# A decoder layer on one core: output projection among the last attention head, cached keys from a later block on

## The chip, the core and the metric

The kernel runs on one core of one Trainium2 chip. The metric is the device time of one execution, in microseconds (us); lower is better. The engines are called PE (TensorE, matmuls), DVE (VectorE), ACT (ScalarE), POOL (GpSimd) and SP (SyncE, which here issues DMAs). Each runs its own instructions in order.

## The reference, cut

One layer of a hybrid decoder, all in float32. For 1,024 prompt tokens (with 16 learned tokens ahead of them), and for 8 decode tokens that each read 4,096 cached keys and values through a page table:

```python
proj = rms_norm(x, ln_mix_pre) @ w_in              # 1024 -> 2560 columns: q, k, v, a, g
u = a * sigmoid(g)
p = softmax(q @ k.T / 8 - slope * distance)        # causal, 4 heads, two maps each
o = (p[map 0] - lam * p[map 1]) @ v                # decode rows: k, v from cache_k, cache_v
conv = silu(layer_norm(causal_depthwise(u, 31)))
mix = concat(rms_norm(o), conv) @ w_out            # the output projection
x = x + rms_norm(mix)
f = (silu(h @ w_gate) * (h @ w_up)) @ w_down       # h = rms_norm(x), FFN width 2816
y = x + rms_norm(f)
```

## The kernel before, in words

Every float32 matmul of the prompt is made of three: operands are split into a rounded high part H and a rest L (`load_split`: a cast on ACT, a subtraction on POOL or DVE), and `mm3` (L148) issues H·H, H·L and L·H, lines 149 to 151.

The program is written as one stream, with the decode tokens' work strewn into the prompt's. Stages in order:

- Input projection (`stripe_ag`, `stripe_q`, `stripe_k`, `stripe_v`), by columns, with the convolution beside it on DVE, ACT and POOL.
- Attention, 32 blocks: `n = 0..31` is head `h = n // 8` and block `i = n % 8` of 128 queries. `attn` makes scores (tile `S`, L507 and L508), takes row minima on DVE (L509, into `nm`), exponentials on ACT (L515), joins the two maps on DVE (L526), transposes on PE (`AT`, L534), copies on ACT (`ats`, `metaT`, L538) and sums over values on PE (`o`, L548). After four blocks the group is normalized (`oh`, L557 to L566; `or` on POOL, L564), and `heads_out` transposes it (`oT`, L571) into `mo`, some blocks later, where `i % 4 == cfg["od"]`.
- Output projection, 8 blocks of 128 tokens. `w_out_load` splits the eight pieces of w_out (`wo0` to `wo7`; ACT cast L138, POOL subtraction L140), two per attention block from block `wo0` on. `c_load` loads a block's inputs (`mx`, `xr`), `c_block` splits them (`mH`, `mL`), runs 48 matmuls into the tiles `mo`, and normalizes. A block calls for `last_head`, the group of head 3 that holds its tokens. From attention block 24 + `c0` on, one output block follows each attention block.
- The FFN: 66 pieces of weights (`w_raw` loads, `w_split` splits: `wr`, `wH`, `wL`), gate, up and down matmuls (`pg`, `pu`, `dn`), the down sums gathered on DVE (L998).

The decode tokens' cached pages come in steps. A step is one pair of pages, 512 KB: a key step (`dec_scores`) loads it, multiplies by the query on POOL (L679) and, later, sums on DVE (L689, `head_sums`); a value step (`dec_values`) loads it for PE (`pv`, L731). There are 128 of each; the first 23 steps are keys, then both alternate. `head_sums` is placed behind a later product: `rlag` says how many products wait. After the 16 key steps of a decode row `dec_max` (DVE L697, L704, POOL L706) and, once `elag` more products are out, `dec_exp` (DVE L711) follow. The steps are dealt out by rates: `rate_b[h]` per attention block from block `db` on, `rate_c` per output block, `rate_d` per slot of the FFN (133 slots, `fill`). When they are through, the decode tokens' own projections (`sample_units`, 81 steps) take `rate_s` per slot.

Page pairs lie in two kinds of buffers. Before the FFN's part begins (`kv_n[1]` false) there are `kv` of them; then `kv` takes turns with the `p` buffers of attention:

```python
        if kv_n[1] and kv_n[0] % 7 < cfg["p"]:
            return slp.tile([P, NKEY], F32, tag="p", name=name, bufs=cfg["p"])
        return slp.tile([P, 1024], F32, tag="kv", name=name, bufs=cfg["kv"])
```

So six of seven go to the six `p` buffers, and each of these comes up again after seven calls.

The order of each engine is fixed when the program is built: a scheduler takes the written stream, its priorities (decode steps may go ahead by `behind`) and data dependences, and puts the instructions of each engine in one row. SP issues nearly all loads, in its own row.

## Time and profile before

| | |
|---|---|
| median of 3 runs | 1452.58 us (1447.33 to 1453.26) |
| the profiled execution, its own time | 1442.33 us |
| its span, first to last instruction | 1440.6 us |
| PE busy | 1353.5 us (94%) |
| DVE, POOL, ACT busy | 876.8, 560.5, 552.2 us |
| mean granted PE clock | 0.976 of full speed |
| DMA moved | 264.35 MB, 183 GB/s over the span |

All durations below come from the profiled execution, which is 10 us under the median of the runs. A matmul's busy time overlaps the next one's, so PE's time is read from where it is idle, and from the granted clock, 1 being the upper of two levels and a mean below 1 a mixture of both. Idle time of another engine matters only where PE waits for it. Names such as `k` or `wH` are the program's tiles; "<-" stands before what they are made from.

### The profile page before, as it was taken

What the parts mean: (1) busy time and instruction counts of PE and PEld (TensorE: products, weight loads), DVE (VectorE), ACT (ScalarE), POOL (GpSimd) and SP (SyncE); (2) the same over time, 40 slices, a digit from 0 to 9 for tenths busy, and PEclk for the clock granted to TensorE, in tenths of its full rate; (3) what the DMA queues carried; (4) which work ended last, traced back from release to release, by engine and by line L of the source; (5) the groups of instructions that cost most, each with busy time, mean ns of one, the idle gap of its engine ahead of it and who ended that gap; (6) DMA issues with size and microseconds to landing.
All of it is one profiled execution on the core that took longest, in us unless ns stands there. A gap on an engine that the chain in (4) does not pass through costs nothing.

```text
span 1440.6 us, 21580 instructions
## 1 busy us (share of the span) xinstructions
PE 1353.5 (94%) x6960; PEld 1054.5 (73%) x6960; DVE 876.8 (61%) x1403; ACT 552.2 (38%) x1112; POOL 560.5 (39%) x351
## 2 busy tenths in 40 slices
PE   5999899979858999999999989999999999999997
PEld 5999799978746787777777667677676765666666
DVE  5689996945765467465748366565754265462158
ACT  7566978697855345212222121222122112211122
POOL 4598866444444123545445455454530000000023
PEclk9999999999979999999999999999999999999999
DMA  8221024226515538678777868687687656664454
GB/s 253 78 59 39 28 64 145 81 88 199 160 61 183 176 125 283 221 241 278 260 244 235 260 202 262 229 273 248 206 267 231 224 159 217 220 202 125 146 190 176
DMA packets 199678, 264.35 MB, mean 183 GB/s; under 512 B 16423, under 2 KB 99816, under 8 KB 199557
## 3 DMA queue, kind: packets, MB, share of 16 engines
q1 hardware_dynamic: 188912, 254.40, 54.1%
q10 hardware_dynamic: 10653, 8.57, 1.9%
q8 instruction: 55, 0.90, 0.3%
q14 instruction: 58, 0.48, 0.1%
HBM read 245.92 MB, written 17.48 MB: 183 GB/s over the span
## 4 chain that ended last, share of the span: by engine, by line
PE 61%; DMA 2%; issue 2%; DVE 2%; SPq 2%; POOL 1%; ACT 0%; POOLq 0%; DVEq 0%; ACTq 0%
PE pg L149 5%; PE pu L149 5%; PE pg L150 5%; PE pu L150 5%; PE pu L151 5%; PE pg L151 5%; PE dn L149 5%; PE dn L150 5%; PE dn L151 5%; PE pv L731 4%; PE mo L151 2%; PE mo L149 2%; PE mo L150 2%; DMA k<-in_cache_k 1%; POOL k L679 1%
## 5 line engine op out<-in xcount | busy, mean ns | idle before, releaser
L679 POOL TENSOR_TENSOR k<-k,qB 128x1024 f32<-128x1024 f32 x128 | 317.8, 2499 | 257.1 <-DMA k<-in_cache_k 212.0
L689 DVE TENSOR_REDUCE s<-k 128x16 f32<-128x1024 f32 x128 | 155.0, 1213 | 106.9 <-POOL k L679 106.8
L955 ACT CAST wH<-wr 128x1024 fp32r<-128x1024 f32 x66 | 69.1, 1049 | 249.1 <-DVE wL L957 142.6
L149 PE MATMUL dn<-wH,aH 128*128 128x512 f32 x352 | 141.2, 405 | 4.4 <-DVE y L998 2.7
L150 PE MATMUL dn<-wL,aH 128*128 128x512 f32 x352 | 140.9, 400 | 0.0
L149 PE MATMUL pu<-hH,wH 128*128 128x512 f32 x352 | 140.3, 399 | 0.5 <-DVE y L998 0.5
L151 PE MATMUL dn<-wH,aL 128*128 128x512 f32 x352 | 140.7, 400 | 0.0
L149 PE MATMUL pg<-hH,wH 128*128 128x512 f32 x352 | 140.4, 399 | 0.0
L151 PE MATMUL pu<-hH,wL 128*128 128x512 f32 x352 | 138.6, 395 | 1.5 <-DVE sm2n_t L123 1.5
L150 PE MATMUL pu<-hL,wH 128*128 128x512 f32 x352 | 139.5, 397 | 0.0
L150 PE MATMUL pg<-hL,wH 128*128 128x512 f32 x352 | 139.3, 396 | 0.0
L151 PE MATMUL pg<-hH,wL 128*128 128x512 f32 x352 | 139.2, 395 | 0.0
L957 DVE TENSOR_TENSOR wL<-wr,wH 128x1024 fp32r<-128x1024 f32 x66 | 97.1, 1471 | 38.0 <-ACT wH L955 21.6
L998 DVE TENSOR_TENSOR y<-dn,y 128x512 f32<-128x512 f32 x144 | 95.0, 684 | 35.4 <-PE dn L151 34.9
L414 POOL TENSOR_TENSOR cb<-cb 128x512 f32<-128x512 f32 x80 | 102.9, 1318 | 17.7 <-ACT cb L413 9.9
L423 DVE SCALAR_TENSOR_TENSOR acc<-u,cw,acc 128x512 f32<-128x512 f32 x144 | 98.8, 749 | 0.2
L1070 POOL TENSOR_TENSOR y<-y,wfpost 128x512 f32<-128x512 f32 x10 | 17.4, 1754 | 205.2 <-ACT ft L1068 205.1
L149 PEld LDWEIGHTS dn<-wH,aH 128*128 128x128 f32 x352 | 67.3, 192 | 31.2 <-DVE y L998 6.2
L981 ACT CAST aH<-sg 128x512 fp32r<-128x512 f32 x44 | 27.3, 621 | 163.2 <-DVE sg L974 163.1
L149 PEld LDWEIGHTS pu<-hH,wH 128*128 128x128 f32 x352 | 66.1, 188 | 27.8 <-issue 12.0
L149 PEld LDWEIGHTS pg<-hH,wH 128*128 128x128 f32 x352 | 66.1, 188 | 27.4 <-issue 11.6
L150 PEld LDWEIGHTS dn<-wL,aH 128*128 128x128 f32 x352 | 66.9, 190 | 25.1 <-issue 10.3
(581 smaller groups left out, 2947.3 us busy)
## 6 DMA issues: line engine op xcount, KB each, us to landing
k<-in_cache_k SPq DMA_DIRECT2D x256, 256.0 KB
v<-in_cache_v SPq DMA_DIRECT2D x256, 256.0 KB
wr<-in_w_gate SPq DMA_DIRECT2D x22, 512.0 KB
wr<-in_w_up SPq DMA_DIRECT2D x22, 512.0 KB
wr<-in_w_down SPq DMA_DIRECT2D x22, 512.0 KB
sd<-in_w_down SPq DMA_DIRECT2D x22, 512.0 KB
sw_gate<-in_w_gate SPq DMA_DIRECT2D x20, 512.0 KB
sw_up<-in_w_up SPq DMA_DIRECT2D x20, 512.0 KB
```

The lines of the kernel that those rows point to most:

```text
L149: T.matmul(out, lhsT=wH, rhs=xH, start=first, stop=False)
L150: T.matmul(out, lhsT=wH, rhs=xL, start=False, stop=False)
L151: mark(T.matmul(out, lhsT=wL, rhs=xH, start=False, stop=last))
L414: G.tensor_tensor(accp, accp, t, op=ALU.add)
L423: V.scalar_tensor_tensor(dst, src, cw[:, ct, k : k + 1], acc, op0=ALU.mult, op1=ALU.add)
L679: x = G.tensor_tensor(kt, kt, qB.unsqueeze(1).to_broadcast([P, 2, 512]), op=ALU.mult)
L689: x = V.tensor_reduce(s.rearrange("p a c -> p (a c)"), kt.rearrange("p a (c d) -> p (a c) d", d=HD), axis=AX.X, op=ALU.add)
L731: x = T.matmul(pv[32 * g : 32 * g + 8, :], lhsT=a[:, q + i, :], rhs=vt[:, i, :], start=q + i < 4, stop=q + i >= NPG - 4, tile_position=(0, ...
L955: S.copy(H[:, :1024], raw[:, :1024])
L957: V.tensor_tensor(L[:, :1024], raw[:, :1024], H[:, :1024].bitcast(F32), op=ALU.subtract)
L981: S.copy(aH, sg)
L998: V.tensor_tensor(y[b][:, ws], o, y[b][:, ws], op=ALU.add)
```

## The change

Only numbers and two conditions change.

- `c0` 7 to 4, four instead of three blocks allowed: the first output blocks follow attention blocks 28, 29, 30 and 31, where one followed block 31. `wo0` 27 to 23: w_out is loaded from attention block 23 on. `od` 1 to 0: a finished group is transposed one block earlier.
- `db` 3 to 16, `rate_b` (1, 1.25, 1, 0.75) to (0, 0, 0.75, 0.75): key steps begin with head 2.
- `rlag` 1 to (1, 2): in the FFN's part sums stand two products behind. `elag` 2 to 3.
- `kv` 4 to 3, and the turn is over `p + kv`, nine, instead of seven: all nine buffers are then used alike. Before the FFN's part there are three instead of four.
- `rate_d` 2.45 to 2.55, `rate_s` 2.2 to 2.3. `w0` 7 to 6: the first FFN weights are loaded and split one output block earlier.

```diff
--- before.py
+++ after.py
@@ -64,7 +64,7 @@
 
     def kv(name):
         kv_n[0] += 1
-        if kv_n[1] and kv_n[0] % 7 < cfg["p"]:
+        if kv_n[1] and kv_n[0] % (cfg["p"] + cfg["kv"]) < cfg["p"]:
             return slp.tile([P, NKEY], F32, tag="p", name=name, bufs=cfg["p"])
         return slp.tile([P, 1024], F32, tag="kv", name=name, bufs=cfg["kv"])
 
@@ -678,7 +678,7 @@
             n = b * NPG // 2 + pg // 2
             x = G.tensor_tensor(kt, kt, qB.unsqueeze(1).to_broadcast([P, 2, 512]), op=ALU.mult)
             products.append((s[:, pg : pg + 2, :], kt))
-            if len(products) > cfg["rlag"]:
+            if len(products) > cfg["rlag"][kv_n[1]]:
                 head_sums(x)
             yield b
 
@@ -1346,7 +1346,7 @@
                     if nwo == 8:
                         c_start()
                         c_load(0)
-        if n >= 24 + cfg["c0"] and ncb < 3:
+        if n >= 24 + cfg["c0"] and ncb < 4:
             c_one(ncb)
             ncb += 1
         if n >= cfg["db"]:
@@ -1382,13 +1382,13 @@
 CFG = dict(
     nb=3, no=1, ns=6, nd=1, nc=2,
     sqv=1, ksp=0, asp=1, sps=1,
-    od=1, kt=0, ho=0,
+    od=0, kt=0, ho=0,
     wd='d',
-    lag=7, rlag=1, elag=2,
+    lag=7, rlag=(1, 2), elag=3,
     xn_g=(), wi_first=1, wi_e=(13, 17), sq=0,
-    behind=-400, w0=7, w1=7, wi_n=1, anchor=1, wi_v=(8, 9, 10, 11, 12), taps=11, conv=400, r2_g=1, hb=5,
-    vgrp=2, fing=5, ml_g=0, fend=22, cst=0, db=3, cn=6, scn=12, wo0=27, wor=2, c0=7,
-    at=8, slabs=35, kv=4, p=6, dve_mul=0, rate_b=(1, 1.25, 1, 0.75), rate_c=1, rate_d=2.45, rate_s=2.2,
+    behind=-400, w0=6, w1=7, wi_n=1, anchor=1, wi_v=(8, 9, 10, 11, 12), taps=11, conv=400, r2_g=1, hb=5,
+    vgrp=2, fing=5, ml_g=0, fend=22, cst=0, db=16, cn=6, scn=12, wo0=23, wor=2, c0=4,
+    at=8, slabs=35, kv=3, p=6, dve_mul=0, rate_b=(0, 0, 0.75, 0.75), rate_c=1, rate_d=2.55, rate_s=2.3,
     ffn_l=lambda nc: nc.vector,
 )
 _INS = [
```

How the rows of three engines move. On PE, where the output projection begins (`mo` its sums, `o` and `S` attention's), before:

```order
L534 MATMUL AT_5388<-ident,p_5339 128x128
L548 MATMUL o_5132<-vm,metaT_116 128x128
L548 MATMUL o_5132<-V_4108,ats_5378 128x128 x3
L149 MATMUL mo_5430<-wo4H,mH_5420 128x512
L150 MATMUL mo_5430<-wo4L,mH_5420 128x512
L149 MATMUL mo_5457<-wo4H,mH_5420 128x512
L150 MATMUL mo_5457<-wo4L,mH_5420 128x512
```

and now:

```order
L548 MATMUL o_4748<-V_3705,ats_4733 128x128 x3
L548 MATMUL o_4748<-V_3705,ats_4739 128x128 x2
L149 MATMUL mo_4771<-wo4H,mH_4761 128x512
L150 MATMUL mo_4771<-wo4L,mH_4761 128x512
L149 MATMUL mo_4798<-wo4H,mH_4761 128x512
L150 MATMUL mo_4798<-wo4L,mH_4761 128x512
L507 MATMUL S_0_4866<-R_30_4010,L_30_3784 128x392
L508 MATMUL S_0_4866<-R_30_4012,L_30_3784 128x392
```

Before, `mo` begins inside the last sums of block 31 (`ats_5378` is its first part). Now it begins behind the sums of block 28 (`ats_4733`, `ats_4739`), and the scores of block 29 (`S_0_4866`) follow its first rows.

On SP, the loads ahead of the first output block (`k` key pages, `mx` and `xr` the block's inputs, `wpost` a norm's weights; page-table reads and second halves of a pair left out), before:

```order
L665 DMA k_14_5067<-in_cache_k 128x512
L132 DMA wo7r<-in_w_out 128x1024
L665 DMA k_16_5218<-in_cache_k 128x512
L107 DMA wpost<-in_ln_mix_post 128x1024
L107 DMA wffn<-in_ln_ffn_pre 128x1024
L886 DMA xr_5313<-in_x_prompt 128x1024
L886 DMA xr_5418<-in_x_prompt 128x1024
L884 DMA mx_5309<-mixT 128x3x128
L884 DMA mx_5310<-mixT 128x4x128
```

and now:

```order
L884 DMA mx_4588<-mixT 128x3x128
L884 DMA mx_4589<-mixT 128x4x128
L132 DMA wo6r<-in_w_out 128x1024
L665 DMA k_12_4517<-in_cache_k 128x512
L665 DMA k_14_4594<-in_cache_k 128x512
L132 DMA wo7r<-in_w_out 128x1024
L665 DMA k_16_4676<-in_cache_k 128x512
L107 DMA wpost<-in_ln_mix_post 128x1024
L107 DMA wffn<-in_ln_ffn_pre 128x1024
L886 DMA xr_4592<-in_x_prompt 128x1024
L886 DMA xr_4759<-in_x_prompt 128x1024
L884 DMA mx_4755<-mixT 128x3x128
```

The first block's `mx` moved ahead of three key pairs; `wo7` stands behind two key pairs instead of one, and the second block's inputs (`mx_4755`) behind a third.

On DVE, in the FFN, at the end of one decode row's keys (L697 adds the distances, L704 takes the maximum, L711 subtracts POOL's maximum over partitions), before:

```order
L689 TENSOR_REDUCE s_10450<-k_30_11674 128x16
L982 TENSOR_TENSOR aL_11671<-sg_11480,aH_11670 128x512
L697 TENSOR_TENSOR s_10450<-s_10450,dbias 128x256
L704 TENSOR_REDUCE dm_11729<-s_10450 128x8
L711 TENSOR_TENSOR s_10450<-s_10450,dg_11731 128x264
L716 TENSOR_REDUCE dsum<-s_10450 128x8
```

and now:

```order
L689 TENSOR_REDUCE s_10613<-k_30_11801 128x16
L998 TENSOR_TENSOR y_7008<-dn_12030,y_7008 128x512
L697 TENSOR_TENSOR s_10613<-s_10613,dbias 128x256
L689 TENSOR_REDUCE s_11860<-k_0_11861 128x16
L998 TENSOR_TENSOR y_7009<-dn_12038,y_7009 128x512
L704 TENSOR_REDUCE dm_12001<-s_10613 128x8
L998 TENSOR_TENSOR y_7010<-dn_12046,y_7010 128x512
L957 TENSOR_TENSOR wL_12527<-wr_12330,wH_12525 128x1024
L711 TENSOR_TENSOR s_10613<-s_10613,dg_12003 128x264
L998 TENSOR_TENSOR y_7011<-dn_12054,y_7011 128x512
```

The three stood together; now sums of the next row (L689), gathering of down sums (L998) and a weight split (L957) lie between.

## Rows read from the trace of the kernel before

**Rows 1.** The page, part 1: busy us, share of the span, instructions.

```profile
PE 1353.5 (94%) x6960; PEld 1054.5 (73%) x6960; DVE 876.8 (61%) x1403; ACT 552.2 (38%) x1112; POOL 560.5 (39%) x351
```

**Rows 2.** Busy time of each engine by stage, then granted clock, DMA share, GB/s.

```profile
252.00:384.00 132.00, 118.07 (x796) 112.21 (x795) 81.59 (x204) 107.96 (x261) 57.69 (x37) 0.97 0.37 117
384.00:456.00 72.00, 44.30 (x260) 38.52 (x259) 46.66 (x105) 40.59 (x112) 32.64 (x16) 0.79 0.46 151
456.00:549.00 93.00, 93.00 (x436) 74.36 (x435) 52.91 (x93) 34.67 (x91) 18.23 (x19) 1.00 0.49 159
549.00:1140.00 591.00, 582.43 (x2697) 415.77 (x2696) 341.20 (x381) 129.22 (x181) 252.75 (x108) 0.99 0.75 247
1140.00:1405.00 265.00, 259.51 (x1213) 170.27 (x1213) 125.47 (x183) 51.29 (x81) 11.58 (x10) 0.99 0.54 179
```

**Rows 3.** The same table, head 3 in three stretches.

```profile
384.00:408.00 24.00, 15.16 (x85) 13.81 (x84) 18.62 (x51) 13.58 (x37) 6.37 (x4) 0.79 0.55 188
408.00:432.00 24.00, 10.86 (x50) 8.49 (x49) 15.83 (x37) 12.44 (x31) 15.07 (x7) 0.64 0.17 55
432.00:456.00 24.00, 18.28 (x130) 16.22 (x129) 12.21 (x17) 14.57 (x46) 11.20 (x5) 0.93 0.64 210
```

**Rows 4.** List of waits, PE, 384 to 456 us: total, times, longest.

```profile
PE S L507 <- DVE nm L509: 12.7, 4, 5.2
PE oT L571 <- ACT oh L566: 7.8, 2, 5.5
```

**Rows 5.** Timelines in head 3 (start, duration, [idle before <-releaser]): DVE; POOL; SP; PE.

```profile
413.27 1.22 DVE L689 TENSOR_REDUCE s<-k 128x16 f32<-128x1024 f32 x1 [5.75 <-POOL k L679]
...
415.94 4.78 DVE L526 SCALAR_TENSOR_TENSOR p<-p,cc,p 128x400 f32<-128x400 f32 x2
...
408.57 2.37 POOL L140 TENSOR_TENSOR wo2L<-wo2r,wo2H 128x1024 fp32r<-128x1024 f32 x1 [7.95 <-ACT oh L560]
...
415.51 2.35 POOL L140 TENSOR_TENSOR wo3L<-wo3r,wo3H 128x1024 fp32r<-128x1024 f32 x1
418.23 2.34 POOL L140 TENSOR_TENSOR wo4L<-wo4r,wo4H 128x1024 fp32r<-128x1024 f32 x1 [0.36 <-POOL wo3L L140]
...
416.06 0.34 SPq L132 DMA_DIRECT2D wo7r<-in_w_out  x1
435.73 1.16 SPq L665 DMA_DIRECT2D k<-in_cache_k  x2
...
444.52 0.47 PE L571 MATMUL oT<-ident,oh 128*128 128x128 f32 x1 [5.46 <-ACT oh L566]
```

**Rows 6.** The chain of waits in the output projection: start, duration.

```profile
458.64 0.46 PE mo L151 x2
```

**Rows 7.** The products of the cached keys (L679) by stage.

```profile
252.00:384.00 132.00, 33.08 (x14) 0.97 0.37 117
```

**Rows 8.** List of waits, PE, 252 to 384 us.

```profile
PE o L548 <- ACT metaT L538: 6.0, 2, 5.7
PE S L507 <- DVE nm L509: 2.3, 3, 1.1
```

**Rows 9.** One line, L623: durations min/median/max, first and last start.

```profile
L623 PE MATMUL sq<-swq,xsT x16: 592/592/597, 62.1 to 63.4; 128*8 128x512 f32 x16
```

**Rows 10.** List of waits, all engines, 549 to 1140 us.

```profile
POOL k L679 <- DMA k<-in_cache_k: 180.8, 46, 9.2
...
DVE s L689 <- POOL k L679: 98.0, 38, 6.7
...
DVE s L711 <- POOL dg L706: 43.0, 7, 7.9
```

**Rows 11.** Timeline, DVE, at a turn of decode rows; the stage table there.

```profile
828.98 0.43 DVE L711 TENSOR_TENSOR s<-s,dg 128x264 f32<-128x264 f32 x1 [7.93 <-POOL dg L706]
...
828.00:864.00 36.00, 31.34 (x137) 21.91 (x136) 21.90 (x27) 9.40 (x13) 17.92 (x8) 0.91 0.62 202
```

**Rows 12.** One line, L526: durations min/median/max, first and last start.

```profile
L526 DVE SCALAR_TENSOR_TENSOR p<-p,cc,p x52: 347/635/2955, 167.5 to 440.2; 128x400 f32<-128x400 f32 x24, 128x144 f32<-128x144 f32 x4, 128x272 f32<-128x272 f32 x4, 128x128 f32<-128x128 f32 x4
```


## Prediction

> **What bounds the kernel now.** I read the page's engine shares first: TensorE is busy 1353.5 of 1440.6 us [rows 1], so only what PE spends idle, or at the lower of its two clock levels, can be won. Then the table by stage: PE is solid in the projections and FFN, and loses most in one place. Between 252 and 384 us (heads 1 and 2, the opening of head 3) it is busy 118.07 of 132, between 384 and 456 (head 3) only 44.30 of 72, then 93.00 of 93 in the output projection, 582.43 of 591 in the FFN beside the cached pages, and 259.51 of 265 beside the decode tokens' own projections [rows 2]. The idle time there is 13.9, 27.7, 0, 8.6 and 5.5 us.
>
> Head 3 loses twice. [...] Head 3 could give back 27.7 + 8.4 = 36.1 us if PE always had something to do. It waits there for VectorE's row minima (12.7 us) and for ScalarE's scaling of a finished group (7.8) [rows 4]. Behind the minima stands the cached-key work: a sum on VectorE came 5.75 us late because its product stood on POOL behind a w_out subtraction, and then a pair of updates L526 took 4.78 us while POOL did two such subtractions [rows 5].
>
> **Output projection moved into head 3.** One block is 48 matmuls of 512 columns at 0.23 us each [rows 6], 11.1 us. In the new order PE begins block 0 after attention block 28 instead of inside block 31, and finishes blocks 0 to 3, 44 us, before the last weighted sum of block 31. That is more than the 36.1 us to be filled, and the same amount leaves the solid stretch behind. But what PE loses before block 28 is done stays reachable by the old causes: of the 27.7 us idle, only the wait of 5.46 us at 444.5 [rows 5] lies after it, with the last stretch's clock loss (0.07 of 48 us at 76%, halved: 1.3). Lower bound: 7 us; upper bound 36.1. The eight w_out casts and subtractions now must all be done before the first block, on the same ACT and POOL, and four key products stand among them where three did; the reduction over partitions that held VectorE in head 3 is no longer there. I take 15, nearer the lower end, because the causes before block 28 remain. The blocks' own chain (three casts, three subtractions, two multiplications, two normalizations) is now queued among attention's minima on VectorE; it is covered as long as PE has mo to run. If that cover fails, the result is the first rival.
>
> **Keys from the 17th block on.** Steps before the FFN fall from 37 (5 + 10 + 8 + 6 in the attention blocks, 8 in the output blocks) to 20 (6 + 6 + 8). Between 252 and 384 us that takes away 14 products, 33.1 us of POOL [rows 7], with their sums on VectorE. PE waited there 6.0 us for ACT and 2.3 for the minima [rows 8]; ACT is busy 108 of 132 us and does not change. Bounds: 0, since nothing is added there, and 6.3 (the waits for minima and the clock's lack, 0.03 of 132 us). I take 3. Three buffers instead of four before the FFN push the fourth page of the decode tokens' query weights behind its first matmul, which ran at 62.1 us [rows 9]; its matmuls now stand 28 projection matmuls later. Bounds 0 and 5 (one transfer wholly waited for); I take 1, as the order leaves it a cover. The early first FFN weights and head 3's earlier transposes I cost at nothing: PE is solid from 456 to 549, and the loads lie beside that.
>
> **The FFN.** 17 more steps go into it, 236 instead of 219, at 2.55 a slot instead of 2.45: 92.5 slots instead of 89.4. The 81 steps of the decode tokens then take 35.2 slots instead of 36.8, together 127.8 of 133, so the end has cover left. The value steps among them cost PE what they cost before, elsewhere. Nine more products at about 2.5 us on a POOL that is busy 252.75 of 591 [rows 2] cost nothing by themselves. What the stage loses comes through VectorE's queue. It stood 98.0 us before sums whose product was not ready and 43.0 us before the subtraction that waits for POOL's maximum, seven times, at most 7.9 [rows 10]; evictions and buffer releases stand behind these. The largest shows the whole chain: 7.93 us of waiting at 829, then a 36 us stretch with PE at 31.34 and a clock of 0.91 [rows 11]. The change moves each sum one product further back, puts evictions and weight splits between maximum and subtraction, and turns over nine page buffers where seven were in turn. Upper bound: 8.6 idle and 0.09 of 36 us, 3.2, together 11.8. Lower bound: a loss of 8.6, the idle time doubled, since keys are already late from DMA 46 times (180.8 us in all, [rows 10]) and the pages come 4% denser. I take 7: the waits that go are the ones on the chain, and two more buffers are in flight.
>
> **The sum.** 15 + 3 - 1 + 7 = 24 us. Against the profiled execution, 1442.33 us (span 1440.6 and 1.7 around it), that is 1418.3. This execution lies 10.25 us under the median of the runs shown, 1452.58, and the forecast is made for the median: **1428.6**. The ends of the terms give -6.6 (7 + 0 - 5 - 8.6) and 54.2 (36.1 + 6.3 + 11.8).
>
> **The VectorE and POOL collision.** L526 takes 635 ns at the median and 2955 at most [rows 12], and its slow cases are those beside a POOL subtraction [rows 5]. POOL ran 20 us of these in head 3. If each of the eight holds a VectorE instruction by the difference, 2.3 us, 18.6 us of head 3 stay lost however much mo there is; the first term falls from 15 to its lower bound, 7, the total to 16, the time to 1436.6. [...] I give this case 0.08.
>
> **The rivals.** (1) **The feed of the blocks is late, 0.18.** SP issues in order. After wo7's load at 416.06 it stood until 435.73, 19.7 us, before a key load whose buffer a VectorE sum had to release [rows 5], and everything the first output block reads stood behind it. In the new order wo7's load stands behind two key loads and block 1's inputs behind a third, with one buffer fewer. If that wait recurs, mo starts where it started before and the first term is 0: 1452.6 - (0 + 3 - 1 + 7) = 1443.6. For it: the same in-order wait. Against it: the sums it needs now stand before block 28's work on VectorE, and block 0's inputs are ahead of these keys. (2) **Everything fills, 0.12**: 36.1 + 6.3 + 11.8 = 54.2, or 1398.4. For it: 44 us of work for 36; against: the waits before block 28. (3) **The FFN pays, slower, 0.09.** Each of the seven turns from one decode row to the next costs what the worst did, 36 - 31.34 + 3.2 = 7.9 us, 55 in all against 11.8 now: 43 more, less the 17 of the other terms, 1478.6. It decides once keys arrive later than the buffers look ahead: then VectorE waits at the sum however far back it stands. For it: 180.8 us of waiting for key transfers; against: DMA is busy 75% there [rows 2]. That the change would not do what it says is excluded: the order is fixed when the kernel is built, and shows it.
>
> **The numbers.** The forecast has 0.53, the collision 0.08, the rivals 0.18, 0.12 and 0.09. About 0.5% (7.3 us) is what a measurement here can tell from no change. Faster by more: forecast, collision, rival 2 and half of rival 1, which gains 9: 0.80 after 0.02 for a low draw of the forecast; the rest of rival 1 and that draw make 0.11 the same, rival 3 0.09 slower. The range 1404 to 1447 holds the forecast with its bounds, the collision and rival 1, and leaves out rival 3 and the far end of rival 2.
>
> **What the changed profile would show.** The first term is right if PE's idle time in head 3 falls from 27.7 to about 14 with the clock back near 1, mo rows between S rows, and the first FFN matmul some 17 us earlier than 549. The FFN term is right if VectorE's wait before L711 is mostly gone and PE's idle time beside the pages is under 3 us. Rival 1 would show as an SP wait of 15 us or more before a key load in head 3, with the first mo still after its end. I am wrong altogether if the FFN stage grows by more than the value steps moved into it, or if head 3 keeps its 27 us.

## The result, and the profile after

The changed kernel took 1473.81 us (median, 1468.11 to 1477.29), the kernel before 1452.38 beside it. The ratio of the runs is 1.0173, 95% interval 1.0148 to 1.0198 (the two medians alone give 1.0148). It is slower by 21 us where 24 us faster was forecast, and outside the range. The profiled execution has a span of 1466.4 us, 25.8 over that of before.

The stages, in the table of busy time by stretch (columns as in [rows 2]: length, busy time of PE, PEld, DVE, ACT and POOL, PE's granted clock, DMA share, GB/s):

```profile
252.00:384.00 132.00, 118.68 (x796) 113.81 (x794) 67.27 (x186) 109.36 (x267) 36.09 (x27) 0.96 0.29 90
384.00:456.00 72.00, 54.51 (x274) 47.30 (x275) 52.14 (x93) 36.88 (x97) 40.85 (x21) 0.86 0.47 161
456.00:504.00 48.00, 46.05 (x234) 37.77 (x233) 30.48 (x62) 22.95 (x59) 17.86 (x14) 1.00 0.55 181
504.00:540.00 36.00, 26.58 (x118) 21.32 (x117) 22.15 (x46) 12.91 (x35) 7.96 (x8) 0.86 0.29 91
540.00:576.00 36.00, 34.39 (x161) 27.08 (x160) 26.17 (x32) 14.16 (x28) 15.99 (x8) 0.99 0.75 241
...
615.00:1175.00 560.00, 541.85 (x2488) 383.51 (x2490) 327.05 (x347) 111.56 (x146) 247.06 (x103) 0.98 0.75 247
1175.00:1453.00 278.00, 267.48 (x1271) 179.33 (x1264) 143.19 (x213) 55.12 (x93) 23.14 (x20) 0.99 0.56 189
```

Head 3 moved the way that was forecast, though less far: 17.5 us idle instead of 27.7 [rows 2], where 14 was forecast, a granted clock of 0.86 instead of 0.79, where near 1 was, and the first output block at 421.3 us instead of 451.5. But the stretch from 504 to 540, solid before, now has 9.4 us idle and a clock of 0.86. How the two kernels stand at the first and the last down matmul shows the rest (one line's instructions of tile `dn`: duration in ns, then first and last start), before and after:

```profile
L149 PE MATMUL dn<-wH,aH x352: 387/395/793, 613.6 to 1431.6; 128*128 128x512 f32 x176
```

```profile
L149 PE MATMUL dn<-wH,aH x352: 387/393/505, 614.9 to 1453.0; 128*128 128x512 f32 x176
```

The first `dn` comes 1.3 us later, the FFN takes 838.1 us instead of 818.0, and 13.4 instead of 9.0 us follow the last one. The forecast's sign, the first FFN matmul (`pg`) some 17 us earlier, came at 536.8 us, 12.1 earlier; but 44 matmuls of the output projection now follow it, where none did, so the first `dn` is the fairer sign.

For a sum I take PE's **loss** in a stage: its idle time plus what the clock lacks (1 minus the granted clock, times the length), added over slices of 12 us. Idle time at the lower clock counts in both parts, so it is a rough measure. (Of the 2,880 slices of 0.5 us up to 1440 us of the kernel before, 2,737 have a clock of 1.00 and 121 of 0.50; the other 22 lie between.) What is left of a stage is work at full clock, and that hardly differs: 1320.4 us before, 1318.9 after, up to the last `dn`. (Over all the runs below it lies between 1312 and 1329, so a few us of loss in one profile say little.) The losses are the change:

| stage | before | after |
|---|---|---|
| 0 to 384 | 47.5 | 46.1 |
| 384 to first `dn` | 42.9 | 47.4 |
| first `dn` to last `pv` (beside the pages) | 12.0 | 26.6 |
| last `pv` to last `dn` | 8.9 | 13.9 |
| behind the last `dn` (time) | 9.0 | 13.4 |

These add 27.1 us, less 1.5 of work: the 25.8 measured, within rounding.

The timelines between 506 and 536 us show the first new stop (start, duration, engine, line, operation, in brackets the idle time before it and what ended it), POOL first, then DVE, ACT and PE:

```profile
506.82 2.42 POOL L679 TENSOR_TENSOR k<-k,qB 128x1024 f32<-128x1024 f32 x1 [2.44 <-DMA k<-in_cache_k]
515.85 0.40 POOL L706 PARTITION_ALL_REDUCE dg<-dm  x1 [6.61 <-issue]
523.39 0.59 POOL L125 TENSOR_TENSOR zr_r<-zr_t,mhalf 128x1 f32<-128x1 f32 x1 [7.15 <-issue]
...
516.27 0.43 DVE L711 TENSOR_TENSOR s<-s,dg 128x264 f32<-128x264 f32 x1 [3.03 <-POOL dg L706]
524.02 1.29 DVE L913 SCALAR_TENSOR_TENSOR xr<-z,zr_r,xr 128x1024 f32<-128x1024 f32 x1 [4.55 <-POOL zr_r L125]
...
525.39 1.06 ACT L916 ACTIVATE z<-xr 128x1024 f32<-128x1024 f32 x1 [6.54 <-DVE xr L913]
...
530.75 1.08 PE L872 MATMUL hT<-ident,z 128*128 128x128 f32 x4 [5.25 <-DVE hL L877]
534.90 0.80 PE L149 MATMUL mo<-wo4H,mH 128*128 128x512 f32 x1 [3.08 <-ACT mH L899]
```

This is the turn of the first decode row. The all-reduce on POOL works for 0.40 us, but POOL stands 6.61 us ahead of it and 7.15 us behind it, waiting for nothing that the profile names. Behind it stands `zr_r`, which the normalization of an output block needs; DVE, ACT and PE wait down the chain. In the kernel before, the all-reduce of that row stood in head 3. Its POOL timeline there:

```profile
390.53 2.35 POOL L140 TENSOR_TENSOR wo1L<-wo1r,wo1H 128x1024 fp32r<-128x1024 f32 x1 [1.73 <-ACT wo1H L138]
400.22 0.40 POOL L706 PARTITION_ALL_REDUCE dg<-dm  x1 [7.34 <-issue]
```

The next on POOL is the subtraction `wo2L` at 408.57 [rows 5]: from 392.9 us to there POOL worked for 0.40. The source view of L706, after, shows two changes of POOL's configuration ahead of each of the eight all-reduces, 6 to 8 us before it starts; the views of L679 and L125 show two more behind each, before the next ordinary instruction.

```profile
L706 POOLq MODIFY_POOL_CONFIG  x16: 4/12/33, 509.2 to 1115.3; - x16
L706 POOL PARTITION_ALL_REDUCE dg<-dm x8: 393/395/396, 515.8 to 1121.0; - x8
L679 POOLq MODIFY_POOL_CONFIG  x12: 108/108/108, 634.8 to 1056.8; - x12
L125 POOLq MODIFY_POOL_CONFIG  x4: 108/108/108, 516.2 to 1121.4; - x4
```

POOL stands idle for 5.9 to 8.1 us ahead of each of the eight all-reduces of this kernel, and for 6.9 to 7.8 us behind each of the first seven (it had no work behind the eighth).

In the FFN the first turn runs on as follows; POOL, DVE, ACT and PE between 622 and 652 us, after:

```profile
625.78 2.38 POOL L679 TENSOR_TENSOR k<-k,qB 128x1024 f32<-128x1024 f32 x1 [1.17 <-DMA k<-in_cache_k]
634.50 0.40 POOL L706 PARTITION_ALL_REDUCE dg<-dm  x1 [6.34 <-issue]
642.38 10.30 POOL L679 TENSOR_TENSOR k<-k,qB 128x1024 f32<-128x1024 f32 x4 [7.49 <-issue]
...
644.75 1.22 DVE L689 TENSOR_REDUCE s<-k 128x16 f32<-128x1024 f32 x1 [2.56 <-POOL k L679]
647.09 1.22 DVE L689 TENSOR_REDUCE s<-k 128x16 f32<-128x1024 f32 x1 [1.12 <-POOL k L679]
648.22 5.54 DVE L957 TENSOR_TENSOR wL<-wr,wH 128x1024 fp32r<-128x1024 f32 x2
...
642.02 1.18 ACT L743 COPY pvs<-pv 8x512 f32<-8x512 f32 x2 [6.20 <-PE pv L731]
...
644.74 1.04 ACT L955 CAST wH<-wr 128x1024 fp32r<-128x1024 f32 x1 [0.34 <-ACT pvs L743]
...
645.84 0.50 PE L149 MATMUL pu<-hH,wH 128*128 128x512 f32 x1 [3.94 <-ACT wH L955]
650.50 0.80 PE L151 MATMUL pu<-hH,wL 128*128 128x512 f32 x1 [2.90 <-DVE wL L957]
```

The two waits of PE have different causes. The second, 2.90 us, hangs on the all-reduce: no product for 14 us, so late sums, and a weight split `wL` behind them on DVE. The split was slow besides, 5.54 us for two beside POOL's products. The first, 3.94 us, does not: PE waits for a cast `wH` that ACT's row has behind the four copies of a finished row of values (`pvs`, L743), and these waited for PE's own last `pv`. With the all-reduce taken out (e9 below) this wait stays; with 2.45 steps a slot (e3) the cast stands ahead of the copies, and PE does not wait for it:

```profile
633.92 0.79 PE L149 MATMUL pu<-hH,wH 128*128 128x512 f32 x1 [3.93 <-ACT wH L955]
```

```profile
636.37 1.04 ACT L955 CAST wH<-wr 128x1024 fp32r<-128x1024 f32 x1
642.43 1.18 ACT L743 COPY pvs<-pv 8x512 f32<-8x512 f32 x2 [5.03 <-PE pv L731]
```

The waits of DVE from 500 to 1200 us answer to [rows 10]:

```profile
DVE s L711 <- POOL dg L706: 50.8, 8, 10.5
DVE s L689 <- POOL k L679: 34.3, 18, 6.7
```

The sums wait a third of what they did (98.0), as forecast; the subtraction behind the all-reduce does not wait less (50.8, against 43.0 in seven of its eight places before).

### The profile page after: what moved, and what is told of

Its sections match the earlier page's. It is cut to its first block, busy times and chain, and to the rows that moved or that the text cites. A ratio compares the mean times of both kernels' runs of the same rounds, so it can differ in the third digit from the quotient of the medians.

```text
span 1466.4 us, 21588 instructions
## 1 busy us (share of the span) xinstructions
PE 1358.9 (93%) x6960; PEld 1060.1 (72%) x6960; DVE 883.4 (60%) x1403; ACT 552.3 (38%) x1112; POOL 565.3 (39%) x351
## 4 chain that ended last, share of the span: by engine, by line
PE 56%; DVE 11%; issue 6%; DMA 6%; ACT 4%; SPq 3%; POOL 2%; ACTq 0%; DVEq 0%; POOLq 0%
PE pg L150 5%; PE pg L151 5%; PE pg L149 5%; PE pu L151 4%; PE pu L149 4%; PE pu L150 4%; PE pv L731 4%; PE dn L149 3%; PE dn L151 3%; PE dn L150 3%; DMA v<-in_cache_v 2%; PE o L548 2%; SPq L665 2%; SPq L659 2%; DMA k<-in_cache_k 1%
## 5 line engine op out<-in xcount | busy, mean ns | idle before, releaser
L679 POOL TENSOR_TENSOR k<-k,qB 128x1024 f32<-128x1024 f32 x128 | 322.5, 2536 | 268.3 <-DMA k<-in_cache_k 189.7
L689 DVE TENSOR_REDUCE s<-k 128x16 f32<-128x1024 f32 x128 | 153.5, 1209 | 44.1 <-POOL k L679 44.1
L957 DVE TENSOR_TENSOR wL<-wr,wH 128x1024 fp32r<-128x1024 f32 x66 | 106.9, 1622 | 77.1 <-PE pg L150 27.7
L998 DVE TENSOR_TENSOR y<-dn,y 128x512 f32<-128x512 f32 x144 | 96.9, 683 | 43.6 <-PE dn L151 43.3
L414 POOL TENSOR_TENSOR cb<-cb 128x512 f32<-128x512 f32 x80 | 102.5, 1314 | 19.5 <-ACT cb L413 11.6
L974 DVE TENSOR_TENSOR sg<-sg,pu 128x512 f32<-128x512 f32 x44 | 30.0, 681 | 119.7 <-PE pu L151 119.6
L1070 POOL TENSOR_TENSOR y<-y,wfpost 128x512 f32<-128x512 f32 x10 | 14.2, 1427 | 194.8 <-ACT ft L1068 194.8
L150 PEld LDWEIGHTS pg<-hL,wH 128*128 128x128 f32 x352 | 67.4, 191 | 27.3 <-issue 12.9
```

Source lines behind the costliest of these rows:

```text
L150: T.matmul(out, lhsT=wH, rhs=xL, start=False, stop=False)
L414: G.tensor_tensor(accp, accp, t, op=ALU.add)
L679: x = G.tensor_tensor(kt, kt, qB.unsqueeze(1).to_broadcast([P, 2, 512]), op=ALU.mult)
L689: x = V.tensor_reduce(s.rearrange("p a c -> p (a c)"), kt.rearrange("p a (c d) -> p (a c) d", d=HD), axis=AX.X, op=ALU.add)
L957: V.tensor_tensor(L[:, :1024], raw[:, :1024], H[:, :1024].bitcast(F32), op=ALU.subtract)
L974: V.tensor_tensor(sg, sg, o, op=ALU.mult)
```

## The experiments

The numbers of all runs in one table: median of the runs, ratio to the kernel before on the same chip with its interval, then PE's losses as above (384 to first `dn` | beside the pages | last `pv` to last `dn`) and the time behind the last `dn`. Single profiles lie up to 6 us from their medians, that of the kernel before 10 us under its own.

| run | us | ratio | losses | behind |
|---|---|---|---|---|
| before | 1452.38 | | 42.9, 12.0, 8.9 | 9.0 |
| after | 1473.81 | 1.0173 (1.0148 to 1.0198) | 47.4, 26.6, 13.9 | 13.4 |
| e1 old FFN settings | 1471.87 | 1.0182 (1.0130 to 1.0234) | 53.8, 28.3, 9.0 | 15.8 |
| e2 FFN settings alone | 1445.55 | 0.9988 (0.9958 to 1.0019) | 36.2, 26.2, 6.1 | 8.5 |
| e3 rate 2.45 | 1449.94 | 1.0039 (1.0011 to 1.0066) | 48.1, 8.6, 12.1 | 15.8 |
| e4 turn later | 1462.74 | 1.0121 (1.0067 to 1.0175) | 38.7, 31.0, 10.4 | 15.9 |
| e5 rate 2.65 | 1462.94 | 1.0096 (1.0075 to 1.0116) | 44.2, 30.1, 11.0 | 9.5 |
| e6 2.45, old lags | 1459.91 | 1.0076 (1.0050 to 1.0102) | 56.2, 16.4, 9.6 | 15.7 |
| e7 2.45, old turn of buffers | 1466.68 | 1.0132 (1.0095 to 1.0168) | 45.5, 30.3, 8.0 | 15.8 |
| e8 2.45, turn later | 1467.97 | 1.0131 (1.0106 to 1.0156) | 42.0, 23.7, 23.6 | 15.9 |
| e9 after, no all-reduce | 1439.20 | 0.9954 (0.9934 to 0.9975) | 33.8, 5.6, 13.6 | 13.4 |
| e10 before, no all-reduce | 1420.18 | 0.9811 (0.9769 to 0.9852) | 27.4, 0.0, 11.2 | 9.0 |
| e11 2.45, maximum by PE | 1436.37 | 0.9935 (0.9912 to 0.9958) | 32.3, 4.7, 8.1 | 15.7 |
| e12 before, maximum by PE | 1424.76 | 0.9845 (0.9808 to 0.9883) | 26.7, 0.0, 9.2 | 9.4 |
| e13 2.65, turn shifted | 1466.23 | 1.0122 (1.0093 to 1.0151) | 40.8, 32.5, 13.2 | 13.7 |
| e14 rate 2.40 | 1456.78 | 1.0057 (1.0036 to 1.0077) | 43.6, 30.3, 5.4 | 11.4 |
| e15 rate 2.50 | 1459.15 | 1.0067 (1.0042 to 1.0093) | 42.8, 27.6, 11.8 | 11.0 |
| e16 e12 and FFN settings | 1418.67 | 0.9787 (0.9762 to 0.9812) | 32.1, 0.0, 7.3 | 8.7 |
| e17 after, maximum by PE, 3.0 | 1443.84 | 0.9990 (0.9971 to 1.0010) | 36.9, 9.2, 13.6 | 9.5 |
| e18 e16 and two blocks in head 3 | 1417.55 | 0.9814 (0.9780 to 0.9848) | 21.1, 6.0, 6.8 | 8.5 |

### One half of the change alone (e1, e2)

e1 is the changed kernel with

```diff
-    rlag=(1, 2), elag=3, rate_d=2.55
+    rlag=(1, 1), elag=2, rate_d=2.45
-        if kv_n[1] and kv_n[0] % (cfg["p"] + cfg["kv"]) < cfg["p"]:
+        if kv_n[1] and kv_n[0] % 7 < cfg["p"]:
```

> The changed kernel with the old lags (sums one product behind, the subtraction after two more), the old turn of seven over the page buffers and the old rate of 2.45 steps a slot; output projection in head 3, keys from the 17th block on, and so 236 steps in the FFN, stay. Theory A (what costs is that 17 more steps stand in the FFN and the first row's turn stands in the output projection): the stage from the first dn to the last dn stays 14 us or more over the 818.0 us of before, the idle 9 us of PE between 504 and 540 stay, time 1464 to 1476. Theory B (what costs is the longer lag and the buffers held longer, which make the weight splits late): the stage falls to about 822 us (818 and 7 more value steps of 0.53 us), time 1454 to 1460.

The stage from first to last `dn` took 835.3 us and the time was 1471.87, both as theory A has it; B fell. The stop in the output projection was even longer with the old lags, one wait of 13.97 us in PE's timeline:

```profile
526.95 0.77 PE L149 MATMUL mo<-wo4H,mH 128*128 128x512 f32 x1 [13.97 <-ACT mH L899]
```

e2 is the kernel before with `kv=3`, the turn over nine, `rlag=(1, 2)`, `elag=3`, `rate_d=2.55`, `rate_s=2.3`.

> The kernel before with only the FFN's settings of the change: turn over nine buffers (three of them of the extra kind), sums two products behind, the subtraction after three more, 2.55 steps a slot and 2.3 after. Keys begin in block 3 as before, so 219 steps are left for the FFN, and the output projection stays behind head 3. Theory A (number of steps in the FFN): the stage from first to last dn stays within 5 us of 818.0, time 1447 to 1458. Theory B (lag and buffers): the stage takes 830 to 838, weight splits wait as in the changed kernel (about 4 us of PE before wH and 3 before wL), time 1464 to 1474.

822.7 us from first to last `dn`, within A's 5 us of 818.0, and 1445.55 us, 1.5 under A's range and far from B's. The table shows it is not that simple: beside the pages it loses 26.2 us, as the changed kernel does, and has it back from smaller losses and less work elsewhere. So it does not take 17 more steps to make that loss.

### Rate, and the place of the first turn (e3, e4)

e3 is the changed kernel with `rate_d=2.45`; e4 with `rate_c=0`.

> The changed kernel with 2.45 steps a slot in the FFN instead of 2.55. If the density of the pages is what starves PE (theory A, first form): PE idle between the first pg and the last pv falls from 21 to about 10 us, time 1460 to 1466. If it is the lag, the buffers or the number of steps: idle time stays near 21, time 1471 to 1477.

> The changed kernel with no decode steps in the output blocks (12 key steps before the FFN instead of 20, 244 in it), so that the first decode row's turn (maximum over partitions, exponentials) falls into the FFN instead of the output projection. Theory A (the turn there stops PE, 9.4 us idle and a clock of 0.86 between 504 and 540): that stretch becomes solid and the first pg comes 9 to 12 us earlier, at 525 to 528; of that the 8 steps more in the FFN cost a part, time 1464 to 1470. Rival: the stop lies elsewhere (late inputs of the blocks): first pg stays at 535 to 538, time 1474 to 1482.

e3 took 1449.94, below what either theory gave, with a loss of 8.6 us beside the pages. e4 moved the first `pg` from 536.8 to 524.1 us, 12.7 earlier, with nothing lost from 504 to it: the turn was the stop there. But the turn then stood in the FFN's first slots, which lost 11.6 us ahead of the first `dn` and 31.0 beside the pages. The time is 11 us below the changed kernel's by the medians, the span only 5.4.

### Rate, lags and buffers one by one (e5 to e8)

e5: `rate_d=2.65`. e6: `rate_d=2.45` with `rlag=(1, 1)`, `elag=2`. e7: `rate_d=2.45` with the turn `% 7`. e8: `rate_d=2.45`, `rate_c=0`, `rate_s=2.5`.

> The changed kernel with 2.65 steps a slot instead of 2.55 (2.45 took 1449.94). Density theory (each step more per slot makes the value pages and weight splits later, so idle time grows with the rate): PE idle and clock loss between the first dn and the last pv rise from 18.1 + 8.5 to 30 us or more, the stage from first to last dn takes 845 us or more, time 1478 to 1490. Phase theory (2.55 only happens to put a row's turn beside a weight split at 645 and 910 us): idle time as likely falls as rises, the stage takes 820 to 835, time 1455 to 1470.

> 2.45 steps a slot as in the run that took 1449.94, buffers in turn over nine, but the old lags: sums one product behind, the subtraction after two more. If the longer lag pays (as the prediction had it: VectorE waits for products no longer), the old lag brings VectorE's wait before the sum back from about 35 to 95 us and the stage from first to last dn from 817.6 to 830 or more, time 1462 to 1472. If the lag is neutral and the turn over the buffers is what pays: stage 816 to 822, time 1448 to 1455.

> 2.45 steps a slot and the long lags as in the run that took 1449.94, but the old turn, six of seven loads into the attention's buffers and one into the three others. If the buffers in flight are what pays: seven usable buffers instead of nine, one product more held back, so value pages come late (PE waits on v at every row's turn, 3 to 5 us each as in the run with both old), stage 832 or more, time 1464 to 1474. If the lag pays: stage 816 to 822, time 1448 to 1455.

> 2.45 steps a slot, no decode steps in the output blocks (12 keys before the FFN, 244 steps in it), and 2.5 steps a slot for the decode tokens' own projections so that they end before the last block. If the two effects add: first pg at 526 instead of 538.9 (12 us), stage near 818, of 15.8 us behind the last dn some 5 less: 1449.9 - 12 + 4 (eight more value steps and a new turn in the FFN) - 5 = 1437, or 0.5% under the kernel before. If the turn in the FFN costs there what it cost in the output projection: 1448 to 1455.

e5 fits neither whole: the loss of 30.1 us is the density theory's, the time of 1462.94 the phase theory's, and the stage of 838.1 us lies between them. The time comes from an earlier first `dn` (610.6) and 9.5 us instead of 13.4 at the end. e6 cost 10 us more than e3, but its stage, 821.3 us, is that of a neutral lag: the cost came from a stop of 13.76 us in the output projection (8.3 in e3, in two waits) and 16.4 instead of 8.6 beside the pages. e7 lost 30.3 there. So e3 needs both new settings, and e1, with neither, is no worse than e7. e8 failed: the two gains did not add, and 1467.97 is 31 us over what was expected and above the second range too. At this point nothing explained why losses jumped between 9 and 31 us; most of the larger stops stood within 35 us behind an all-reduce, one for each decode row (in the changed kernel all five of PE's stops of 2 us or more between 504 and 1175 us, 11 to 20 us behind one).

### The turn without GpSimd's all-reduce (e9 to e12)

e9 (on the changed kernel) and e10 (on the kernel before):

```diff
-        G.partition_all_reduce(mg, m, P, bass.bass_isa.ReduceOp.max)
+        G.tensor_copy(mg, m)
```

Both leave out the maximum over partitions: each partition keeps its own.

> The changed kernel with GpSimd's maximum over all partitions replaced by a GpSimd copy of each partition's own maximum, so the maximum over partitions is left out (the decode tokens' weights are then shifted by a different number in each partition). What goes with it are the 6 to 8 us in which GpSimd stands ahead of each of eight such instructions and the 7 us behind. Theory T (the turn from one decode row to the next is what costs, because these 14 us hold up products, sums, buffer releases and, in the output projection, the normalization of a block): the 9.4 us of idle time and 3.3 of clock before the first pg go, and of 28.7 + 11.9 between first and last dn 15 to 25 go; time 1436 to 1452. Rival P (phase or density of the transfers, whatever POOL does): only the part before the first pg goes, time 1458 to 1466.

> The same replacement in the kernel before (the maximum over partitions is left out). Its turns stood in head 3 once, where PE idled anyway, and in the FFN seven times, where idle and clock loss between first and last dn are 14.1 + 6.8. Theory T: it gains much less than the changed kernel does, 4 to 14 us, 1434 to 1446, so that the 21 us between the two kernels shrink to 10 or less. Rival P: it gains 0 to 4 us and the two stay 15 us or more apart.

e9 is within theory T's range and 35 us under the changed kernel's 1473.81 (by the two ratios, 32), e10 26 under the 1446.06 beside it. Busy time by stretch, e10 and then e9 (columns as above):

```profile
384.00:504.00 120.00, 102.67 (x536) 84.23 (x535) 78.99 (x158) 61.26 (x165) 47.37 (x29) 0.91 0.52 174
602.00:1115.00 513.00, 513.00 (x2380) 366.61 (x2380) 297.05 (x326) 102.87 (x134) 219.35 (x93) 1.00 0.76 252
```

```profile
384.00:504.00 120.00, 101.23 (x510) 86.17 (x511) 82.09 (x155) 60.40 (x160) 59.71 (x35) 0.91 0.51 171
504.00:528.00 24.00, 21.32 (x108) 17.41 (x107) 19.95 (x42) 11.76 (x32) 6.25 (x6) 1.00 0.34 110
603.00:1143.00 540.00, 536.07 (x2488) 381.22 (x2490) 324.75 (x347) 111.92 (x146) 242.82 (x103) 1.00 0.76 256
```

In e10 PE is busy for all of 513 us beside the pages: the 12.0 us that the kernel before loses there are the all-reduces'. Its head 3 loses 27.4 us instead of 42.9, with the output projection still behind it. In e9 the 26.6 become 5.6, which is the wait of 3.93 us before `wH` and the clock behind it. In the traces the instructions of PE, ACT and POOL stand in the same order, by line and tile, in e9 as in the changed kernel, VectorE's in all but 4 of 1,403 places, so it is no other order that wins. That the all-reduces cost is shown: 26 us in the old order, 32 to 35 in the new. The second half of theory T fell: it had e10 gain less, and the two within 10 us; they stay 19 apart (13.9 in the profiles), as rival P had it for this part. So most of the difference between the two orders is not the all-reduces'. Of the 13.9, 8.3 lie between first and last `dn`, 4.4 behind it, and the first `dn` comes at 603.0 and 601.8: without all-reduces, the new order wins nothing ahead of it.

e11 (on e3) and e12 (on the kernel before) compute the same maximum without POOL:

```diff
-        mg = smt(f"dg{b}", 8, 2)
-        G.partition_all_reduce(mg, m, P, bass.bass_isa.ReduceOp.max)
-        st[b] = s, mg
+        mp = po1(f"mp{b}")
+        T.transpose(out=mp[:8, :P], in_=m, identity=ident)
+        mx = smt(f"dx{b}", 8, 2)
+        V.tensor_reduce(mx[:8, :1], mp[:8, :P], axis=AX.X, op=ALU.max)
+        mg = smt(f"dg{b}", 8, 2)
+        V.tensor_scalar(mg[:8], ident[:8, :8], mx[:8, 0:1], None, op0=ALU.mult)
+        T.matmul(mp[:, P : P + 8], lhsT=ones[:8, 0:1].to_broadcast([8, P]), rhs=mg[:8], start=True, stop=True)
+        st[b] = s, mp[:, P : P + 8]
```

> The changed kernel at 2.45 steps a slot (1449.94) with the maximum over partitions on other engines: PE transposes the 128 x 8 maxima, VectorE takes the maximum of each row, and a matmul with ones brings it to all partitions; GpSimd has no part in it. If the turn is what stops PE: before the first pg 13 us go (9.4 idle, 4.1 clock), in the FFN some 5, against at most 8 times 1 us for PE's own waits for VectorE: 1428 to 1440, faster than both kernels. If PE waiting for VectorE in its own order takes its place (8 times 2 to 3 us): 1446 to 1456.

> The kernel before with the same maximum by PE and VectorE. If the turn costs little where it stands in the kernel before: 1440 to 1450, within 0.5% of it. If the turns were half of the 20.9 us that PE loses between first and last dn there: 1434 to 1440.

e11 took 1436.37, 13.6 under e3 and within its first expectation. e12 took 1424.76, 21.3 under the kernel before and below both of its own: these left out the turn in head 3, where the loss falls by 16 us (42.9 to 26.7). For this maximum over partitions, of 128 x 8 and between other work of POOL, the way over PE and VectorE was faster (1424.76 us against 1446.06). PE pays little for its part, though the scheduler also put the engines' rows in another order for it. The row of L706 in e12 (eight transposes) and its stretch beside the pages:

```profile
L706 PE MATMUL mp<-ident,dm x8: 270/271/275, 404.1 to 1060.4; 128*8 128x128 f32 x8
```

```profile
604.00:1121.00 517.00, 517.00 (x2399) 368.00 (x2399) 318.34 (x338) 103.52 (x134) 217.71 (x87) 1.00 0.75 250
```

### Density or place (e13 to e15), and the settings without turns (e16)

e13 is e5 with `rate_c=0`; e14 `rate_d=2.40, rate_s=2.5`; e15 `rate_d=2.50`; e16 is e2 with the maximum by PE.

> 2.65 steps a slot with no decode steps in the output blocks: 8 steps more in the FFN, so every row's turn stands 3 of the 6 slots of a weight block later than in the run with 2.65. There (a turn every 12.08 slots, so always at the same place of a block) PE stopped at the turns for the same thing each time, the down matmuls waiting for VectorE's y. Place theory: the stops are again alike, but of another kind (v pages or weight splits), and the loss between first dn and last pv, 19.8 idle + 10.3 clock there, moves by more than 10 us either way. Density theory: kind and size stay, 26 to 36 us.

> The changed kernel with 2.40 steps a slot (and 2.5 for the decode tokens' projections, so that they end in time). Loss of PE between first dn and last pv was 8.6 us at 2.45, 26.6 at 2.55, 30.1 at 2.65. Density theory: 9 us or less, time 1446 to 1452. Place theory (a turn every 13.33 slots stands elsewhere each time): anything between 5 and 30 us, most likely near the mean of the runs so far, 22, time 1455 to 1468.

> The changed kernel with 2.50 steps a slot. Density theory: the loss between first dn and last pv lies between 8.6 and 26.6 us, time 1452 to 1470. Place theory: it need not; outside these two with an even chance.

> The kernel before with the maximum over partitions by PE and VectorE (1424.76) and, on top, the change's settings of the FFN: nine buffers in turn, sums two products behind, subtraction after three, 2.55 and 2.3 steps a slot. With the turns gone nothing is lost between first dn and last pv, so these settings can win nothing there: 1420 to 1430, the same. If they cost something of their own (denser pages): 1432 or more.

PE's waits beside the pages, e5 and then e13 (us in total, times, longest):

```profile
PE dn L149 <- DVE y L998: 15.8, 5, 5.3
PE pu L149 <- ACT wH L955: 3.9, 1, 3.9
```

```profile
PE pv L731 <- DMA v<-in_cache_v: 10.1, 14, 1.7
PE pu L149 <- ACT wH L955: 9.2, 1, 9.2
PE pg L149 <- ACT wH L955: 4.4, 1, 4.4
```

The kind of stop changed with the place, as the place theory has it; the size did not (32.5 against 30.1). In e13 the casts `wH` stand on ACT behind the exponentials that wait for the all-reduce, so there the 9.2 us hang on it. The sparsest pages lost 30.3 us (e14), so density falls too: by rate the losses are 30.3, 8.6, 27.6, 26.6 and 30.1. e16 shows that the FFN settings cost nothing of their own: 0.0 lost beside the pages, and 1418.67 us, a little under the range expected.

### What is left without turns (e17, e18)

e17 is the changed kernel with the maximum by PE and `rate_s=3.0`; e18 is e16 with `c0=6`, two blocks allowed, `wo0=25`, `od=0`, `w0=6`.

> The changed kernel whole (2.55, all settings) with the maximum over partitions by PE and VectorE, and 3.0 instead of 2.3 steps a slot for the decode tokens' own projections, so that these end some 8 slots earlier and their last work on VectorE no longer stands behind the last block. If the 13 to 16 us behind the last dn (9.0 in the kernel before) come from that: 9 us there, time 1426 to 1434. If they come from the FFN's last sums themselves: 13 us stay, 1434 to 1442. Both say that the change, with the turns gone, stays 8 us or more behind the kernel before with the same maximum and the FFN settings (1418.67).

> The kernel that took 1418.67 (keys from block 3 on, FFN settings of the change, maximum by PE and VectorE) with two blocks of output projection in the last head: transposes one block earlier, w_out from block 25, output blocks after attention blocks 30 and 31, first FFN weights one block earlier. If output blocks fill idle time of PE in head 3 once no turn stands there (18.4 idle and 13.7 clock between 384 and 504): first pg 5 to 12 us earlier than 543.9, time 1407 to 1414. If the loss lies ahead of block 28 and they only change places with the solid stretch: first pg within 3 us, time 1416 to 1422.

In e17 the time behind the last `dn` fell to 9.5 us, where e9 and e11, with 2.3 steps a slot, had 13.4 and 15.7: so that part of the loss was the decode tokens' projections, pushed late. The time did not follow: 1443.84, above both ranges. The 9.2 us lost beside the pages are one wait of 5.67 us at 639.3 us, again for a `wH` behind the `pvs` copies, and the clock behind it. Why the work between first and last `dn` is 803.5 us where e9 has 798.1 stays open. In e18 the first `pg` came at 523.5 instead of 543.9 us, here too with 44 matmuls of the output projection now behind it, and the first `dn` 11.0 us earlier, with 21.1 instead of 32.1 us lost ahead of it. So two blocks in head 3 do fill idle time once no all-reduce stands there; but 7 of these us went again up to the last `dn`, and the time is the second's, that of e16. e11, e12, e16 and e18 beat the two kernels of this study.

## Why the prediction was wrong

**Head 3, forecast 15 us won.** Up to 504 us the losses fell by 13.1 (42.9 to 29.8), which looks like the forecast. But 12.7 came back before the first `pg` and 4.9 behind it: up to the first `dn` the losses rose by 4.5, below the lower bound of 7. Two steps failed. The first is "the reduction over partitions that held VectorE in head 3 is no longer there": it was booked as gone, and not followed to its new place. It was 15.5 of the 42.9 us lost in head 3 (e10), and now stands in the output projection, which the prediction took for solid: 9.4 us idle and 3.3 of clock before the first `pg`. The second is that `mo` would fill what PE loses in head 3: without all-reduces the new order loses 33.8 us up to the first `dn` (e9) and the old one 27.4 (e10), and up to 504 us 29.1 and 27.4. So, as far as single profiles tell, the 13.1 us are the all-reduce going from there, and no filling by the four blocks shows. The prediction had put head 3's waits behind POOL's subtractions [rows 5]; a POOL that waits 7.34 us for nothing and then does 0.40 us of work is on the same timeline, and the next subtraction stood 7.95 us behind it. No run shows the 8.4 us of clock in the upper bound of 36.1, or the 1.3 in the lower, as such. In slices of 0.25 us the clock of 384 to 456 us is 1.00 or 0.50 in 281 of 288 before and in 280 after; in those under 0.75 PE was busy 18.8 us before (3.2 of them in the last stretch) and 15.8 after. Half of that, 9.4 and 7.9 us, is my estimate of what the lower clock cost there.

**Chain of the blocks "covered as long as PE has mo to run".** The cover failed at the all-reduce: `zr_r` behind it, the next block's `hT` and `mH` behind that.

**Keys gone from heads 0 to 2, and the fourth query-weight page, forecast 3 - 1.** Losses up to 384 us fell by 1.4 between these two profiles. Over all the runs they are 48.4 us on average with keys from block 3 on (six runs) and 45.1 with keys from block 16 on (fourteen), which bears the 3 out. Not all 14 products went from the stretch, as the prediction had it: four stay, 9.77 us. Before the matmuls of the query weights (now 60.3 to 67.8 us) PE does not stand idle; the upper bound of 5 us for them was taken from no row.

**FFN, forecast 7 won, lower bound 8.6 lost.** Beside the pages 14.6 us were lost more, behind that 5.0. The mechanism of the lag was right: VectorE's wait for products fell from 98.0 to 34.3 us, and the old lags make the stop in the output projection longer (e1, e6). The step that failed is "the waits that go are the ones on the chain": the chain hung on the all-reduce, where POOL's stop is not shortened by a lag (13.1 to 15.8 us of idle time around an all-reduce before, 12.9 to 15.6 after), and L711's wait did not fall. The all-reduces cost 12.0 us beside the pages before and 21.0 now (26.6 less the 5.6 of e9). The 5.6 are the change's own: a cast `wH` that ACT's new row has behind the copies `pvs`. The loss there is 12.0 us in the kernel before and 8.6 in e3, 16 to 33 in the other runs with the all-reduce. Rate, lags, buffers and number of steps were each changed and none rules it alone; where the cast `wH` falls in ACT's row is one part of it, and the rest is open.

**The end, costed at nothing ("cover left").** 4.4 us more behind the last `dn`; e17 shows that they belong to the decode tokens' projections, which 17 more steps push back. Counted as the prediction counts slots, the runs agree: where these projections end by slot 126 of the 133, 8.5 to 9.5 us follow the last `dn`, and 11.0 to 15.9 where they end at 127 to 132. So 127.8 of 133 was no cover.

**All of it.** The all-reduces cost both orders nearly alike, so they explain why the forecast gain did not come more than why the change is slower. Without them the new order is still behind by 19 of the 21 us by the medians, by 1.43 of 1.73% by the ratios, by 13.9 of 25.8 us by single profiles. The 13.9 are placed by the losses of e9 and e10: 6.4 ahead of the first `dn`, 5.6 at `wH`, 2.4 behind the last `pv` and 4.4 at the end, less 5 by which these profiles differ before 384 us and in the work. Only the 4.4 were taken away by an experiment; for the others the place is shown and the cause argued. The prediction's own bounds reached 1459.2 on the slow side, its range 1447; the result is beyond both.

**Value steps, costed at nothing.** Right: PE's work in all is the same within 1.5 us in the two profiles.

**The rivals.** (1) did not occur: SP waited 1.4 us for sums of keys between 384 and 540 us, and the first `mo` came at 421.3. (2) did not either. (3) had the side and nearly the time (1478.6), but not the cause, so its number is near by luck: waits of products for key transfers between 500 and 1200 us fell, from 189.0 us to 173.5, and an all-reduce cost 3.0 us beside the pages (21.0 by seven), not 7.9. The collision of VectorE with POOL was not tried by itself. L526 has its median of 635 ns as before [rows 12], but the weight split `wL`, 1.2 us at the median, is slower than 1.35 in 14 of 66 places before and 21 after, up to 3.4 us, each time beside an instruction of POOL; together these lose VectorE 17 us before and 27 after. What that costs PE is open.

## What to carry to other kernels

A short instruction that stands between long idle times "waiting for nothing" was an expensive one here (0.40 us of work, with 13 to 16 us of idle POOL around it): count the idle time on both sides as its price, and follow it to where a change moves it. When much of a stage's loss comes from a few such events, another rate, lag or buffer count deals their cost out anew, over a span of 24 us here (1449.94 to 1473.81); taking the event away (8 all-reduces, 21 us of 1446) was worth more than any other order tried with it in place. Compare losses stage by stage: that showed that a gain in head 3 was spent before the FFN. And take the event out of both kernels: only that showed that the new order is slower by itself, and that the gain in head 3 was the event leaving and not the work moved in.

## What the hardware showed that was not expected

GpSimd's all-reduce among its ordinary operations cost twice: in the changed kernel 5.9 to 8.1 us ahead of the all-reduce and 6.9 to 7.8 us behind it, before an ordinary instruction, for 0.40 us of work. The transpose on PE that takes its place is 0.27 us, and with it, VectorE's reduction and a small matmul PE had no idle time beside the pages (e12, e16). PE's granted clock beside the pages was 1.00 where it had no stops (e10, e12), and 0.99 before and 0.98 after, where it had; in e3 and e9 it was 1.00 too, with 8.6 and 3.9 us idle.
